# Seven products in place of eight for one more quarter of the fifth gate-and-up block

## The chip, the cores and the metric

The kernel runs on one NeuronCore of one Trainium2 chip. The metric is the device time of one execution in microseconds, taken as the median of several runs. TensorE (PE) multiplies matrices, VectorE (DVE) and ScalarE (ACT) do the elementwise work, GpSimd (POOL) issues some of the DMAs, and SyncE (SP) issues most of them.

## The reference

One layer of a streaming encoder on 256 rows of width 2048, all in 32-bit floats: a gated feed-forward network (FFN), a mixing part (a state-space group beside an attention group), a second FFN and a gated embedding. The change touches the first FFN's gate and up products only:

```python
def rms_norm(x, gain):
    xf = x.astype(jnp.float32)
    y = xf * lax.rsqrt(jnp.mean(xf * xf, axis=-1, keepdims=True) + EPS)
    return (y * gain.astype(jnp.float32)).astype(x.dtype)

def swiglu(h, w_gate, w_up, w_down):
    return (jax.nn.silu(h @ w_gate) * (h @ w_up)) @ w_down

x = x + 0.5 * swiglu(rms_norm(x, ffn1_norm[i]), ffn1_w_gate[i], ffn1_w_up[i], ffn1_w_down[i])
```

Here h is 256 x 2048 and each of w_gate and w_up is 2048 x 5632.

## The kernel before

**Blocks and quarters.** `ffn` goes over the 5632 columns in 11 blocks of 512 (`f` = 0 to 10). A block needs, for gate and for up, the product of 256 rows (two tiles `t` of 128) with 2048 x 512 weights. The depth of 2048 is taken in four quarters of 512 rows; one DMA of 1 MB brings a quarter of one weight into a `raw` buffer (five of them, in turn).

**Split operands.** Each operand is written as a high and a low part. ACT casts a half of a quarter (256 rows of depth) to the high part `whi`, and DVE subtracts to get the low part `wlo` (`split`, L182 and L185). For each 128 rows of depth PE adds three matmuls: high times high, low activations times high weights, high activations times low weights. A half of a quarter for both row tiles is thus 2 x 2 x 3 = 12 matmuls of 128 x 128 by 512 columns. `weight_pair` hands out the pairs of `whi` and `wlo`: four of them before the seventh block.

**Plain blocks.** `gemm_block` runs the four quarters of gate, then the four of up, each half by `gemm_half` (L353, L358), and calls `step()` after each half: 16 steps in a block.

**Seven products.** For one quarter, gate and up taken together form a 2 x 2 arrangement of weight blocks (`b11`, `b21` the two halves of gate's quarter, `b12`, `b22` those of up's). The two row tiles and the two halves of depth form the other 2 x 2 arrangement, and the kernel multiplies the two with seven block products in place of eight, each of six matmuls (L539, L542, L544 in `Seven.multiply`). That needs sums of the weight blocks on DVE (`t1`, `t2`, `t4`, L550), one sum `b12 + b22` that an accumulating DMA on POOL's queue makes in place (L578), sums of activations made once per quarter (`sum_forms`), and additions of the results at the end. `Seven.single` is the form that uses single banks of accumulators: products 1, 6 and 7 share one bank, so that the bank is copied out to `one` (L585, on ACT) before product 6 begins in it, and `six` (L595) and `seven` (L114, the line of `put_off`) are formed on DVE from it. In the blocks named in `alone`, the first quarter goes through `single` and the other three through `column`, gate first, then up: 4 + 6 + 6 = 16 steps as well. After gate's columns `gated` adds up the gate (L723, L726; the activation on ACT is L724). After up's columns `ended` adds the double bank of products 3 and 8 (L752) and multiplies gate and up (L754, twice). In a plain block that last multiplication is L792, twice.

**What comes beside.** `step()` advances every generator in `beside` once: the state-space preparation `s5_prep` (its lines are some 900 to 1160: L1087 to L1131 on DVE, L1115 on PE, coefficient loads L1071 and stores L1143 on POOL's queue), and whatever `put_off(n, ...)` has set for n steps later. In a block by sevens `ended` is put off to the next step, which is the first step of the block after it.

**Buffers.** `com("sg")` is one buffer of 1024 columns, `com("h")` two. In a block by sevens `sg` holds first the copy `one` and then the gate, and `h` the two halves of up. PSUM gives four single banks (`acc`) and two double ones (`aux`); the preparation's small products also use `aux`.

**Order.** Each engine runs its instructions in one order that the framework's scheduler fixes when the kernel is built; `pin` keeps program order for some of them, and `tc.issue_after` sets one behind another.

```python
early = 6 if bg else 0
alone = (3, 5) if bg else ()
```

So in the first FFN blocks 0, 1, 2 and 4 are plain, 3 and 5 have one quarter by sevens, and 6 to 10 have two by `chunk`. `f` counts from 0, and the text counts blocks from one: `f` = 3, 4, 5 are the fourth, fifth and sixth block.

Of the kernel before, what the change touches and what calls it, by code (L numbers as in the profile page):

```python
# [33 lines left out]
def layer_kernel(ctx: ExitStack, tc: tile.TileContext, a: dict, shapes: dict, out: bass.AP):  # L34
# [290 lines left out]
    @contextmanager  # L325
    def sums_phase(name):
        with phase(name) as pool:
            yield pool
            ring[0] = None
# [345 lines left out]
    def ffn(i, xn, nxt, bg=None):  # L675
# [1 line left out]
        hT = []  # L677
        pools = ExitStack()
        early = 6 if bg else 0
        alone = (3, 5) if bg else ()  # L680
        sevens = pools.enter_context(sums_phase(f"sums{i}"))
        hp = pools.enter_context(phase(f"h{i}"))
        side = ExitStack()
# [927 lines left out]

    n1, nm, n2, npl = Normed("ffn1_norm", load_turned), Normed("mix_norm"), Normed("ffn2_norm", kinds="hhnn", late=0), Normed("ple_norm", late=0)
    ffn(1, n1, nm, s5_prep)

    w_in = a["w_in"]
# [75 lines left out]
    mix.close()  # L1691

    ffn(2, n2, npl)


# [254 lines left out]
```

## Time and profile before

| what | value |
|---|---|
| median of 3 runs | 1808.87 us |
| lowest, highest | 1808.36, 1809.96 us |
| profiled execution | 1808.1 us |
| its span | 1806.3 us |
| matmuls | 8890, PE busy 1799.4 us |
| DVE busy | 1615.7 us |
| ACT busy | 1083.6 us |
| weights' and other bytes moved | 430.49 MB, mean 238 GB/s |

The span is the time from the first to the last instruction of the program; the run's time has 1.8 us around it. Busy times of PE count a matmul from its start to its modelled end, and matmuls overlap: their pace is read from the distance of their starts. Rows of the timeline begin with the start in us from the span's start and the duration; a bracket at the end gives the engine's idle time before the instruction and what ended it. In the rows of windows, a number in brackets counts the instructions. The fifth block begins on PE at 181.10 us and the sixth at 225.67 us.

### The profile page before, as it was taken

The page shows a single profiled execution, that of the slowest core. Times are in us where ns is not written, and L with a number is a line of the kernel's source. Part 1 is how long each engine was busy: PE and PEld are TensorE (multiplying, and loading weights), DVE is VectorE, ACT ScalarE, POOL GpSimd, SP SyncE. Part 2 cuts the span into 40 slices and gives each one's busy share as a digit, 9 for nine tenths or more (in the row PEclk, how much of TensorE's full clock was granted, in tenths as well). Part 3 has the DMA queues.
Part 4 walks back from the last instruction along what each step waited for, and adds up shares of the span by engine and source line. Part 5 has one row for each costly group of instructions (what it writes and reads, how often), then busy time and mean ns, then how long its engine had stood idle before and what let it go on. Part 6 is the DMA issues. An engine that isn't in the chain of part 4 may idle for free.

```text
span 1806.3 us, 24268 instructions
## 1 busy us (share of the span) xinstructions
PE 1799.4 (100%) x8890; PEld 1492.0 (83%) x8890; DVE 1615.7 (89%) x1894; ACT 1083.6 (60%) x1263; POOL 134.6 (7%) x196
## 2 busy tenths in 40 slices
PE   9999999999999999999999999999999999999998
PEld 7888888888888888888898888888888888888887
DVE  7998889999999898887867899999999999989875
ACT  7445455555566666466895566555565566666664
POOL 0020100000000001122121000000000000000000
PEclk9999999999999999999999999999999999999999
DMA  9689967687776667765646777776767786666663
GB/s 377 215 280 312 278 219 235 237 273 216 262 253 225 209 245 230 254 243 182 202 153 209 242 284 239 262 261 228 234 233 240 244 273 242 233 210 220 208 245 128
DMA packets 108518, 430.49 MB, mean 238 GB/s; under 512 B 24592, under 2 KB 48432, under 8 KB 66000
## 3 DMA queue, kind: packets, MB, share of 16 engines
q1 hardware_dynamic: 95952, 390.10, 61.1%
q0 software_dynamic: 12160, 38.55, 9.9%
q8 instruction: 69, 1.13, 0.3%
q14 instruction: 49, 0.40, 0.1%
q10 hardware_dynamic: 288, 0.31, 0.1%
HBM read 372.41 MB, written 10.88 MB: 212 GB/s over the span
## 4 chain that ended last, share of the span: by engine, by line
PE 99%; DMA 0%; DVE 0%; ACT 0%; SPq 0%; issue 0%; DVEq 0%; ACTq 0%
PE acc L358 31%; PE acc L353 16%; PE aux L358 15%; PE aux L353 8%; PE acc L539 5%; PE acc L544 5%; PE acc L542 5%; PE aux L544 4%; PE aux L539 4%; PE aux L542 4%; PE aux L1328 0%; PE acc L1585 0%; PE acc L1580 0%; PE acc L1576 0%; DMA raw<-in_head 0%; PE aux L1273 0%
## 5 line engine op out<-in xcount | busy, mean ns | idle before, releaser
L185 DVE TENSOR_TENSOR wlo<-raw,whi 128x1024 fp32r<-128x1024 f32 x478 | 576.4, 1221 | 94.0 <-ACT whi L182 90.7
L182 ACT CAST whi<-raw 128x1024 fp32r<-128x1024 f32 x478 | 495.8, 1050 | 271.2 <-PE acc L358 156.6
L358 PE MATMUL acc<-whi,nhi 128*128 128x512 f32 x852 | 332.7, 392 | 1.0 <-ACT whi L281 0.9
L358 PE MATMUL acc<-whi,nlo 128*128 128x512 f32 x852 | 330.4, 389 | 0.0
L353 PE MATMUL acc<-wlo,nhi 128*128 128x512 f32 x852 | 241.3, 390 | 0.0
L185 DVE TENSOR_TENSOR slo<-raw,shi 128x1024 fp32r<-128x1024 f32 x186 | 226.4, 1217 | 11.6 <-ACT shi L182 11.3
L182 ACT CAST shi<-raw 128x1024 fp32r<-128x1024 f32 x186 | 195.2, 1049 | 51.5 <-DMA raw<-in_ffn_w_down 24.0
L358 PEld LDWEIGHTS acc<-whi,nhi 128*128 128x128 f32 x852 | 159.8, 188 | 35.4 <-ACT whi L281 1.5
L353 PEld LDWEIGHTS acc<-wlo,nhi 128*128 128x128 f32 x852 | 159.7, 188 | 33.8 <-DVE wlo L185 0.4
L182 ACT CAST whi<-sum 128x1024 fp32r<-128x1024 f32 x83 | 87.5, 1054 | 166.2 <-DVE sum L550 154.4
L358 PEld LDWEIGHTS acc<-whi,nlo 128*128 128x128 f32 x852 | 159.9, 188 | 32.6 <-DVE nlo L282 0.2
L182 ACT CAST shi<-sum 128x1024 fp32r<-128x1024 f32 x61 | 64.3, 1053 | 103.8 <-DVE sum L550 99.8
L643 POOL DMA_DIRECT2D raw<-raw x47 | 41.4, 880 | 1032.5 <-DVE sum L550 782.0
L550 DVE TENSOR_TENSOR sum<-sum,raw 128x1024 f32<-128x1024 f32 x96 | 117.1, 1220 | 0.9
L185 DVE TENSOR_TENSOR wlo<-sum,whi 128x1024 fp32r<-128x1024 f32 x83 | 101.2, 1222 | 3.1 <-ACT whi L182 2.2
L358 PE MATMUL aux<-whi,nhi 128*128 128x512 f32 x244 | 95.0, 389 | 0.0
L358 PE MATMUL aux<-whi,nlo 128*128 128x512 f32 x244 | 94.9, 389 | 0.0
L185 DVE TENSOR_TENSOR slo<-sum,shi 128x1024 fp32r<-128x1024 f32 x61 | 74.5, 1221 | 0.7
L353 PE MATMUL aux<-wlo,nhi 128*128 128x512 f32 x244 | 75.1, 389 | 0.0
L550 DVE TENSOR_TENSOR sum<-raw,raw 128x1024 f32<-128x1024 f32 x48 | 58.5, 1220 | 3.6 <-DMA raw<-in_ffn_w_down 3.4
L539 PE MATMUL acc<-whi,hhi 128*128 128x512 f32 x154 | 60.2, 391 | 0.0
L542 PE MATMUL acc<-whi,hlo 128*128 128x512 f32 x154 | 60.0, 389 | 0.0
(420 smaller groups left out, 3531.9 us busy)
## 6 DMA issues: line engine op xcount, KB each, us to landing
raw<-in_ffn_w_down SPq DMA_DIRECT2D x88, 1024.0 KB, 4.9
raw<-in_ffn_w_gate SPq DMA_DIRECT2D x87, 1024.0 KB, 7.4
raw<-in_ffn_w_up SPq DMA_DIRECT2D x87, 1024.0 KB, 5.6
raw<-in_w_in SPq DMA_DIRECT2D x32, 1024.0 KB, 5.2
raw<-raw POOLq DMA_DIRECT2D x50, 512.0 KB, 5.6
raw<-in_w_out SPq DMA_DIRECT2D x16, 1024.0 KB, 5.0
raw<-in_w_ple_gate SPq DMA_DIRECT2D x16, 1024.0 KB, 5.0
hT<-mid SPq DMA_DIRECT2D x160, 64.0 KB, 4.7
```

The costliest lines, as they stand in the source:

```text
L182: copy = nc.scalar.copy(hi, src)
L185: rest = nc.vector.tensor_tensor(out=lo, in0=src, in1=hi.bitcast(F32), op=ALU.subtract)
L353: nc.tensor.matmul(ps[t], lhsT=lh, rhs=lo[:, j, cols], start=False, stop=stop and j == 1)
L358: nc.tensor.matmul(ps[t], lhsT=(ahi, alo)[i][:, 2 * h + j, t * P : (t + 1) * P], rhs=hi[:, j, cols], start=start and j == 0 and i == 0, st ...
L539: nc.tensor.matmul(ps, lhsT=lh[j], rhs=hi[:, j], start=begin and j == 0, stop=False, skip_group_check=joined)
L542: nc.tensor.matmul(ps, lhsT=ll[j], rhs=hi[:, j], start=False, stop=False, skip_group_check=joined)
L544: nc.tensor.matmul(ps, lhsT=lh[j], rhs=lo[:, j], start=False, stop=z in final and j == 1, skip_group_check=joined)
L550: nc.vector.tensor_tensor(out=t, in0=x, in1=y, op=ALU.add)
L643: nc.gpsimd.dma_start(b12, b22, accum_op=ALU.add)
```

## The change

The block with `f` = 4 joins those whose first quarter goes through `single`. It then takes the branch of `f in alone`: `single` on quarter 0, `column(0, (1, 2, 3))`, `column(1, (1, 2, 3))`, `gated` and `ended` as in the fourth and sixth block, in place of `gate(gemm_block(...))`, `gemm_block(...)` and the two L792. Nothing else is edited.

```diff
         early = 6 if bg else 0
-        alone = (3, 5) if bg else ()
+        alone = (3, 4, 5) if bg else ()
```

## The prediction

> **What bounds the kernel now.** I read the page first: the span, the busy shares, the slices, the chain that ended last.
>
> ```profile
> span 1806.3 us, 24268 instructions
> PE 1799.4 (100%) x8890; PEld 1492.0 (83%) x8890; DVE 1615.7 (89%) x1894; ACT 1083.6 (60%) x1263; POOL 134.6 (7%) x196
> DVE  7998889999999898887867899999999999989875
> PE 99%; DMA 0%; DVE 0%; ACT 0%; SPq 0%; issue 0%; DVEq 0%; ACTq 0%
> ```
>
> TensorE is busy for 1799.4 of 1806.3 us and the chain is 99% PE: the sum of the matmuls is the time, and an edit counts only by the matmuls it removes and by the holes it makes between them. VectorE (DVE) is next. Then I cut the stretch around the edit at the block starts: fourth block, fifth (the one that changes), sixth.
>
> ```profile
> core 0: us, PE busy (x) PEld busy (x) DVE busy (x) ACT busy (x) POOL busy (x), PEclk, DMA share, GB/s
> 136.90:181.10 44.20, 44.20 (x315) 36.16 (x314) 38.72 (x48) 22.30 (x29) 4.40 (x9) 1.00 0.97 309
> 181.10:225.70 44.60, 44.60 (x258) 36.69 (x257) 37.65 (x45) 19.30 (x22) 5.33 (x10) 1.00 0.91 277
> 225.70:269.00 43.30, 43.30 (x251) 35.43 (x250) 38.18 (x43) 23.55 (x26) 1.43 (x2) 1.00 0.70 229
> 270.00:350.00 80.00, 80.00 (x355) 66.24 (x354) 77.34 (x75) 46.46 (x50) 3.52 (x4) 1.00 0.74 250
> ```
>
> PE is full in all of them, at a granted clock of 1.00. The fifth block has no products by sevens and takes 44.60 us, the sixth has seven of them and takes 43.30; each holds one insertion of 64 small matmuls of the preparation (the fourth holds two). The last row, of the blocks after, shows DVE at 77.34 of 80.00 us with PE still full: a nearly full DVE does not by itself stop PE.
>
> **The change part by part.** *Products removed.* In the fifth block one quarter of the depth, for gate and up together, is 4 halves of 12 matmuls = 48; it becomes 7 products of 6 = 42. The interval between matmuls is read from starts, not from the busy 0.39 us, because they overlap.
>
> ```profile
> 139.63 0.39 PE L539 MATMUL acc<-whi,nhi 128*128 128x512 f32 x1
> 140.99 0.39 PE L539 MATMUL acc<-whi,hhi 128*128 128x512 f32 x1
> ```
>
> One product of six takes 140.99 - 139.63 = 1.36 us, 0.227 per matmul. Six fewer: -1.36 us. The blocks above agree: 44.60 - 43.30 = 1.30. [...] Six matmuls at the load's 0.188 us would be 1.13 us, and by their busy time 2.34; the spacing lies between, and it decides.
>
> *VectorE work added.* Per-instruction times, from the rows of the neighbours:
>
> ```profile
> L185 DVE TENSOR_TENSOR wlo<-raw,whi 128x1024 fp32r<-128x1024 f32 x15 | 18.2, 1218 | 6.9 <-ACT whi L182 6.9
> L550 DVE TENSOR_TENSOR sum<-sum,raw 128x1024 f32<-128x1024 f32 x2 | 2.4, 1218 | 0.0
> L792 DVE SCALAR_TENSOR_TENSOR h<-acc,sm,sg x4: 741/746/750, 136.9 to 227.4; 128x512 f32<-128x512 f32 x4
> L595 DVE TENSOR_TENSOR h<-acc,sg x2: 652/652/652, 142.9 to 232.7; 128x512 f32<-128x512 f32 x2
> L114 DVE TENSOR_TENSOR h<-acc,h x2: 684/685/686, 149.5 to 235.6; 128x512 f32<-128x512 f32 x2
> L723 DVE TENSOR_TENSOR sg<-acc,h x2: 681/686/691, 165.9 to 252.9; 128x512 f32<-128x512 f32 x2
> L726 DVE TENSOR_TENSOR h<-acc,h x2: 1217/1218/1218, 167.6 to 254.7; 128x1024 f32<-128x1024 f32 x2
> L752 DVE TENSOR_TENSOR h<-aux,h x2: 1218/1218/1218, 182.3 to 269.9; 128x1024 f32<-128x1024 f32 x2
> ```
>
> Seven splits in place of four: 3 x 1.22 = 3.65. The sums t1, t2, t4: 3 x 1.22 = 3.66. The combination: L595 0.65, L114 0.69, two L723 1.37, L726 1.22, L752 1.22 = 5.15; the two closing multiplications are there before (L792) and after (L754) at 0.75 each. Together +12.5 us on DVE, some 11.5 by starts, as one such instruction starts about 1.13 us after another. ACT gains three casts of 1.05 us and one copy and has 25 us free in the block: nothing.
>
> The cover for the 12.5 us is DVE's idle time:
>
> ```profile
> DVE wlo L185 <- ACT whi L182: 7.7, 6, 1.5
> DVE t L1087 <- DMA bc<-in_ssm_bc: 1.6, 1, 1.6
> DVE wlo L185 <- PE aux L1115: 1.5, 1, 1.5
> ```
>
> These waits of DVE between 169 and 231 us sum to 10.8 us, 6.9 of them inside the block. They are no hardship: DVE has done all that four pairs of buffers allow, and waits for PE to free one. Work put there costs nothing. What is short, about 1.7 us and the 1.36 us by which PE needs things earlier, comes out of DVE's lead; preparation work that sits between the splits is not urgent and can slip. So I take 0 for volume, with bounds 0 and 6.9 us (only the block's own idle usable: a shortfall of 5.55, plus 1.36). Nearest is the row of the later blocks with 77.34 of 80.00 and no hole.
>
> *The start of a block after one by sevens.* This is where I expect the cost. A block by sevens leaves its last step (`ended`: L752, then two L754) to the first step of the block after it. The next block's `single` copies bank 1 into `sg` (L585) before its fourth product may overwrite the bank; `sg` is one buffer, so the copy must wait until the last L754 of the block before has read it. Today a plain block precedes each `single`, and only two L792 stand there. The rows at the sixth block's start:
>
> ```profile
> 225.64 1.22 DVE L1124 TENSOR_TENSOR t<-bt,coef 128x1024 f32<-128x1024 f32 x1
> 226.78 1.41 DVE L792 SCALAR_TENSOR_TENSOR h<-acc,sm,sg 128x512 f32<-128x512 f32 x2
> 228.18 1.05 ACT L182 CAST whi<-raw 128x1024 fp32r<-128x1024 f32 x1 [0.31 <-PE acc L542]
> 229.14 0.58 ACT L585 COPY sg<-acc 128x512 f32<-128x512 f32 x1
> 229.77 0.49 PE L539 MATMUL acc<-whi,hhi 128*128 128x512 f32 x1
> PEld acc L539 <- ACT sg L585: 0.3, 1, 0.3
> ```
>
> L792 ends at 228.19, the copy waits for the cast ahead of it on ACT until 229.14, ends at 229.72, and the fourth product follows at 229.77; PE's weight load waited 0.3 us for it and the matmuls lost about 0.13. There is no room left. [...]
>
> The rows at the start of the fifth block, where the closing step of the fourth runs:
>
> ```profile
> 179.93 2.50 DVE L1100 TENSOR_TENSOR t<-ce,s5s 128x512 f32<-128x512 f32 x4
> 182.34 1.22 DVE L752 TENSOR_TENSOR h<-aux,h 128x1024 f32<-128x1024 f32 x1
> 183.47 1.22 DVE L185 TENSOR_TENSOR wlo<-raw,whi 128x1024 fp32r<-128x1024 f32 x1
> 184.61 1.41 DVE L754 SCALAR_TENSOR_TENSOR h<-h,sm,sg 128x512 f32<-128x512 f32 x2
> 181.10 0.39 PE L358 MATMUL acc<-whi,nhi 128*128 128x512 f32 x1
> ```
>
> PE starts the block at 181.10, so the fourth product is due at 181.10 + 3 x 1.36 = 185.18. If DVE keeps this order, L754 ends at 186.02, the copy at about 186.7, and PE loses 1.57. Bounds: 0, if L752 follows PE's end at once and nothing stands between (then L754 ends near 183.9); 2.6, if a 1.05 us cast also stands before the copy. I take 1.57, the order shown. At the sixth block's start L752 comes ahead of what is there: +1.13 by starts, and another 1.13 if a split slips in as at 183.47, less up to 0.95 that the copy spends behind the cast today. So 0.2 to 2.3; I take 0.8, from the lower half, as the cast's wait can overlap.
>
> *The accumulating DMA.* One more 512 KB addition of the up weights on POOL's queue.
>
> ```profile
> 165.28 2.88 POOL L1071 DMA_DIRECT2D coef<-scr_coef  x6
> 195.51 0.96 POOL L1071 DMA_DIRECT2D coef<-scr_coef  x2 [27.35 <-DVE t L1124]
> 214.33 0.92 POOL L578 DMA_DIRECT2D raw<-raw  x1 [12.87 <-DVE vq L1090]
> 143.86 3.90 ACT L182 CAST whi<-raw 128x1024 fp32r<-128x1024 f32 x4 [3.31 <-DMA raw<-raw]
> DMA to landing us min/median/max: 10.2/10.9/11.7
> ```
>
> It takes 10.2 to 11.7 us to land. In the fourth block ACT waited 3.31 us for it without a hole on PE. Here POOL's queue is free from 168.2 to 195.5, and the seventh product is due at 181.10 + 6 x 1.36 = 189.3: issued by about 175 it is in time. Cost 0, bounds 0 and 2. SP's queue: the up quarter is fetched earlier, the number of fetches stays, and at a DMA share of 0.91 there is room.
>
> Sum: -1.36 + 1.57 + 0.8 = +1.0 us. The profiled execution, 1808.1 us with 1.8 around its span, would go to 1809.1; it lies 0.8 below the median of 1808.87, so as a median: **1809.9 us**. The measurement of this kernel tells about 0.2% (3.6 us) from no change, so this is "same".
>
> **The rivals.**
> - *Full gain.* Scheduling puts L752 and L754 directly behind PE's end, the copy is in time at both starts: 1808.87 - 1.36 = 1807.5. For it: the fourth and sixth blocks run with holes of 0.13 us at most. Against: the rows at 182.34 to 186.02.
> - *DVE becomes the bound* (slower). The 12.5 us find only the 6.9 us inside the block; PE waits 6.9 us for low parts of weights, by the end of the sixth block's products: 1808.87 - 1.36 + 6.9 = 1814.4. It decides when DVE's lead of some 8 us is used up and more than 5 us must be waited for. Against: DVE at 97% later, without a hole. [...]
> - *Late addition.* If t1 slides to 176 us, where DVE is idle, b12 lands near 189.6 and the seventh product starts some 2 us late, beside the stalls above: 1811.9.
> - Faster by over 0.2% would need another 2.2 us of holes to vanish; PE has hardly that in this stage.
>
> **How the numbers follow.** Forecast (one or both starts late, 1808.6 to 1811.5) 0.50; full gain 0.28; late addition 0.08; DVE the bound 0.10; anything else 0.04. Range: down to 1806.9, the full gain with the 0.5 us by which single runs lie under the median; up to 1813.2, both starts at their upper bounds (-1.36 + 2.6 + 2.3 = +3.5) and 0.8 for the spread of runs. The likeliest alone: 1808.6 to 1811.5. Faster 0.03, same 0.86, slower 0.11.
>
> **What would show it.** PE rows: 42 matmuls of L539 to L544 in the fifth block, the distance of block starts 43.2 plus a hole. The hole right before the fourth product at both starts, put down to ACT's L585; L754 ending less than 0.7 us before the fourth product is due. DVE's idle time in the block falling from 6.9 to near 0. L578 three times, its third landing before 188. Wrong if the copy is in time (full gain), or if the waits are for `wlo` and go on past the seventh product (DVE).

## The result, and the profile after

The changed kernel took 1813.19 us, the median of 12 runs (1811.42 to 1814.20), against 1808.41 us for 12 runs of the kernel before (1806.92 to 1809.96): a ratio of 1.0026, 95% interval [1.0018, 1.0034]. It is slower by a little more than the 0.2% that a measurement of this kernel tells from no change. The profiled execution took 1812.45 us. Its page first: span, busy shares, VectorE in 40 slices.

```profile
span 1810.6 us, 24277 instructions
...
PE 1801.3 (99%) x8884; PEld 1492.3 (82%) x8884; DVE 1626.5 (90%) x1906; ACT 1085.1 (60%) x1267; POOL 135.2 (7%) x197
...
DVE  7999999999999898887867899999999999989875
```

Six matmuls are gone (8890 to 8884) and DVE has 10.8 us more to do, yet the span grew by 4.3 us. PE's busy time grew with it, by 1.9 us, though it has less to do: some matmuls must stand further apart. The stretches by block, cut at the starts of fourth, fifth, sixth and seventh block and 42 us on (columns as in the prediction: length, busy time and instructions of PE, PEld, DVE, ACT and POOL, granted clock, DMA share, GB/s):

```profile
136.20:180.30 44.10, 44.10 (x316) 36.06 (x315) 42.02 (x51) 22.39 (x29) 5.36 (x10) 1.00 0.99 310
180.30:224.00 43.70, 43.70 (x251) 35.23 (x250) 39.91 (x46) 22.38 (x26) 5.33 (x10) 1.00 0.79 265
224.00:268.00 44.00, 43.09 (x250) 35.12 (x249) 41.91 (x48) 23.72 (x25) 1.44 (x2) 1.00 0.78 248
268.00:310.00 42.00, 40.06 (x171) 32.61 (x170) 38.02 (x38) 21.61 (x24) 1.68 (x2) 0.96 0.70 238
```

The fifth block now has the sixth's number of matmuls (251). PE (first number behind the comma) has no idle time in it, 0.91 us in the sixth block, and 1.94 us in the last row, which no step of the prediction speaks of; there the granted clock fell to 0.96. PE's waits between 180 and 330 us, the total, the number and the longest:

```profile
PE acc L539 <- ACT shi L182: 1.9, 1, 1.9
...
PE acc L539 <- ACT sg L585: 0.9, 1, 0.9
...
PEld acc L539 <- ACT sg L585: 1.7, 2, 1.3
```

The copy to `sg` (L585) is what it waited for at the two starts, and the weight loads (PEld) with it. The larger wait is for `shi`, the high part of a sum of weight blocks. The timeline around the three places:

```profile
181.53 1.22 DVE L752 TENSOR_TENSOR h<-aux,h 128x1024 f32<-128x1024 f32 x1
...
183.80 1.41 DVE L754 SCALAR_TENSOR_TENSOR h<-h,sm,sg 128x512 f32<-128x512 f32 x2
...
185.24 0.59 ACT L585 COPY sg<-acc 128x512 f32<-128x512 f32 x1
...
185.88 0.50 PE L539 MATMUL acc<-whi,hhi 128*128 128x512 f32 x1
...
217.97 1.22 DVE L550 TENSOR_TENSOR sum<-raw,raw 128x1024 f32<-128x1024 f32 x1
...
219.96 0.92 POOL L578 DMA_DIRECT2D raw<-raw  x1 [11.19 <-DVE sum L550]
...
227.26 1.41 DVE L754 SCALAR_TENSOR_TENSOR h<-h,sm,sg 128x512 f32<-128x512 f32 x2
...
229.04 1.05 ACT L182 CAST whi<-raw 128x1024 fp32r<-128x1024 f32 x1 [1.37 <-DMA raw<-raw]
...
230.00 0.57 ACT L585 COPY sg<-acc 128x512 f32<-128x512 f32 x1
...
230.62 0.50 PE L539 MATMUL acc<-whi,hhi 128*128 128x512 f32 x1 [0.92 <-ACT sg L585]
...
268.72 1.22 DVE L752 TENSOR_TENSOR h<-aux,h 128x1024 f32<-128x1024 f32 x1 [0.24 <-PE aux L353]
...
270.99 1.41 DVE L754 SCALAR_TENSOR_TENSOR h<-h,sm,sg 128x512 f32<-128x512 f32 x2
...
272.32 1.22 DVE L550 TENSOR_TENSOR sum<-sum,raw 128x1024 f32<-128x1024 f32 x1
...
273.62 1.04 ACT L182 CAST shi<-sum 128x1024 fp32r<-128x1024 f32 x1 [5.63 <-issue]
...
274.71 0.50 PE L539 MATMUL acc<-shi,nhi 128*128 128x512 f32 x1 [1.94 <-ACT shi L182]
```

At the fifth block's start L754, the copy and product 6 stand one right behind the other (the last L754 ends at 185.21, the copy starts at 185.24), as predicted; product 6 is 0.15 us late. At the sixth block's start another wait ends last. There L754 was done at 228.67, and product 6 was due at 229.55, so a copy of 0.57 us right behind L754 would have been in time. But on ACT the copy stands behind a cast, and this cast waited for the sixth block's accumulating DMA (`raw<-raw`), which was issued at 219.96 and landed at 228.94. In the kernel before, that DMA went out at 214.33: it waits for `t1`, which DVE made 5.4 us earlier there.

```profile
212.54 1.22 DVE L550 TENSOR_TENSOR sum<-raw,raw 128x1024 f32<-128x1024 f32 x1
```

DVE did not lack the time for `t1` in the new kernel: its weights had landed at 212.76, and DVE was idle for 2.12 and 1.49 us ahead of the two splits that stand before it. `t1` has a later place in DVE's order.

The third group is the seventh block. DVE is not late there, since it waits 0.24 us for PE before L752; but it makes `t4` (L550) only after it has ended the sixth block. ACT has been idle for 5.63 us when it can cast `t4`, and product 4 begins 1.94 us late. In the kernel before, DVE made `t4` ahead of that end:

```profile
265.20 2.48 DVE L550 TENSOR_TENSOR sum<-sum,raw 128x1024 f32<-128x1024 f32 x2
...
268.44 1.06 ACT L182 CAST shi<-sum 128x1024 fp32r<-128x1024 f32 x1
...
269.90 1.22 DVE L752 TENSOR_TENSOR h<-aux,h 128x1024 f32<-128x1024 f32 x1
```

The two L550 of the first row are `t2` and `t4`; `t4` is ready at 267.7 and cast at 268.44, with no wait of PE.

To put sizes on this, take every matmul of 512 columns and add up by how much the distance to the next start exceeds 0.227 us (distances that exceed it by less than 0.013 us are left out). The whole difference of the spans is then there:

| lost PE time, us | before | after | difference |
|---|---|---|---|
| start and rest of the fifth block (183.5 to 227) | 0.22 | 0.78 | +0.56 |
| sixth block (227 to 266) | 0.32 | 1.39 | +1.07 |
| seventh and start of the eighth (266 to 330) | 0.00 | 3.81 | +3.81 |
| everywhere else | 6.2 | 6.5 | +0.3 |

+5.7 us of these and -1.36 us of removed products make +4.3. Of the 3.81, 2.2 are the wait for `t4`, and 1.6 the matmuls right behind it, which stood up to 0.427 us apart.

### The profile page after: what moved, and what is told of

Same layout as the page of the kernel before. It is cut to its first block, busy times and chain, and to the rows that moved or that the text cites. A ratio compares the mean times of both kernels' runs of the same rounds, so it can differ in the third digit from the quotient of the medians.

```text
span 1810.6 us, 24277 instructions
## 1 busy us (share of the span) xinstructions
PE 1801.3 (99%) x8884; PEld 1492.3 (82%) x8884; DVE 1626.5 (90%) x1906; ACT 1085.1 (60%) x1267; POOL 135.2 (7%) x197
## 4 chain that ended last, share of the span: by engine, by line
PE 94%; DVE 2%; DMA 2%; issue 1%; ACT 1%; SPq 1%; POOL 0%; ACTq 0%; DVEq 0%; POOLq 0%
PE acc L358 29%; PE acc L353 15%; PE aux L358 14%; PE aux L353 7%; PE acc L539 5%; PE acc L544 5%; PE acc L542 5%; PE aux L544 3%; PE aux L542 3%; PE aux L539 3%; DMA raw<-in_ffn_w_down 1%; SPq L233 1%; DMA raw<-raw 0%; DVE wlo L185 0%; PE aux L1328 0%
## 5 line engine op out<-in xcount | busy, mean ns | idle before, releaser
L358 PE MATMUL acc<-whi,nhi 128*128 128x512 f32 x812 | 317.4, 393 | 0.1
L358 PE MATMUL acc<-whi,nlo 128*128 128x512 f32 x812 | 314.8, 389 | 0.0
L353 PE MATMUL acc<-wlo,nhi 128*128 128x512 f32 x812 | 231.3, 389 | 0.0
L358 PEld LDWEIGHTS acc<-whi,nhi 128*128 128x128 f32 x812 | 152.5, 188 | 32.6 <-issue 0.5
L353 PEld LDWEIGHTS acc<-wlo,nhi 128*128 128x128 f32 x812 | 152.4, 188 | 31.7
L358 PEld LDWEIGHTS acc<-whi,nlo 128*128 128x128 f32 x812 | 152.6, 188 | 31.1
L550 DVE TENSOR_TENSOR sum<-sum,raw 128x1024 f32<-128x1024 f32 x98 | 119.5, 1220 | 0.9
L185 DVE TENSOR_TENSOR wlo<-sum,whi 128x1024 fp32r<-128x1024 f32 x86 | 105.0, 1221 | 5.6 <-ACT whi L182 4.8
L358 PE MATMUL aux<-whi,nhi 128*128 128x512 f32 x268 | 104.5, 390 | 0.0
L358 PE MATMUL aux<-whi,nlo 128*128 128x512 f32 x268 | 104.3, 389 | 0.0
L353 PE MATMUL aux<-wlo,nhi 128*128 128x512 f32 x268 | 82.5, 389 | 0.0
L550 DVE TENSOR_TENSOR sum<-raw,raw 128x1024 f32<-128x1024 f32 x49 | 59.7, 1219 | 6.3 <-DMA raw<-in_ffn_w_down 5.4
```

The costliest lines, as they stand in the source:

```text
L185: rest = nc.vector.tensor_tensor(out=lo, in0=src, in1=hi.bitcast(F32), op=ALU.subtract)
L353: nc.tensor.matmul(ps[t], lhsT=lh, rhs=lo[:, j, cols], start=False, stop=stop and j == 1)
L358: nc.tensor.matmul(ps[t], lhsT=(ahi, alo)[i][:, 2 * h + j, t * P : (t + 1) * P], rhs=hi[:, j, cols], start=start and j == 0 and i == 0, st ...
L550: nc.vector.tensor_tensor(out=t, in0=x, in1=y, op=ALU.add)
```

## The experiments

Each kernel was timed beside the kernel before on its chip. The table has, for every profile, the lost PE time as above (each of the first two columns holds some 0.2 us of the insertions of small matmuls), and where `t4` of the seventh block stands on DVE against the end of the sixth block. The lost time is that of one execution, the profiled one, which for e1 and e9 was the shortest of the kernel's runs and for e10 the longest (1812.69 us).

| kernel | median, us | minus before, us | ratio, 95% interval | lost 183.5 to 266 | lost 266 to 330 | `t4` |
|---|---|---|---|---|---|---|
| before | 1808.41 | | | 0.5 | 0.0 | ahead |
| after | 1813.19 | +4.8 | 1.0026 [1.0018, 1.0034] | 2.2 | 3.8 | behind |
| e1 | 1807.71 | -0.6 | 0.9998 [0.9989, 1.0008] | 0.9 | 0.0 | ahead |
| e2 | 1814.20 | +5.9 | 1.0031 [1.0020, 1.0042] | 3.8 | 2.9 | ahead |
| e3 | 1814.01 | +5.7 | 1.0032 [1.0019, 1.0045] | 4.2 | 2.2 | behind |
| e4 | 1809.38 | +1.1 | 1.0006 [0.9997, 1.0015] | 2.5 | 0.0 | ahead |
| e5 | 1807.24 | -0.7 | 0.9997 [0.9988, 1.0006] | 0.4 | 0.0 | ahead |
| e6 | 1813.62 | +5.7 | 1.0032 [1.0020, 1.0045] | 3.6 | 4.9 | behind |
| e7 | 1808.82 | +0.9 | 1.0006 [0.9997, 1.0014] | 2.0 | 1.1 | ahead |
| e8 | 1807.83 | -0.1 | 1.0004 [0.9995, 1.0013] | 1.1 | 1.1 | ahead |
| e9 | 1811.25 | +3.5 | 1.0024 [1.0014, 1.0034] | 1.9 | 2.2 | behind |
| e10 | 1810.33 | +2.6 | 1.0015 [1.0007, 1.0024] | 2.9 | 3.8 | behind |
| e11 | 1809.62 | +1.5 | 1.0008 [0.9999, 1.0017] | 4.5 | 0.0 | ahead (set) |
| e12 | 1808.50 | +0.3 | 1.0003 [0.9994, 1.0012] | 2.0 | 1.2 | behind (set) |

**The copy's wait taken away (e1), and the same in the kernel before (e5).** In the blocks by sevens the first product is copied into the single-purpose buffer `sq`, which is free there, and `sg` holds the gate alone. The copy then waits for no earlier block. e5 has the same edit in the kernel before.

```diff
+                one = com("sq") if f in alone else gate_cols[0]
+
-                def gated(s, g=gate_cols, u=up_cols, hh=hh):
-                    for z, (ps, other) in enumerate(((s.bank(2), g[0]), (s.bank(4), u[1]))):
+                def gated(s, g=gate_cols, u=up_cols, hh=hh, one=one):
+                    for z, (ps, other) in enumerate(((s.bank(2), one), (s.bank(4), u[1]))):
...
-                    s.single(0, gate_cols[0], *up_cols)
+                    s.single(0, one, *up_cols)
```

> The changed kernel with the copy of bank 1 (L585) written to another buffer (sq) than the gate's, so that it no longer waits for the two L754 of the block before. Theory A (each hole has its own cause: the copy behind L754 at the fifth and sixth block's start, and at the seventh block's start a split that is planned late): the holes at 185.5 (0.15 and 0.11), about 0.3 around 189 and 229.3 (1.08 and 0.11) go, some 1.5 us, and the 2.1 us at 272.4 with the slow matmuls after it stays: 1811.7 us. Theory B (VectorE has too much to do, and whatever is freed at one place is lost at the next wait): nothing or hardly anything, 1813 us, with the holes moved.

> The kernel before (fifth block plain) with the copy L585 written to the buffer sq. Theory A (the gain of the run with the copy in sq came from the wait that it takes away): here only the 0.13 us at the sixth block's start can go, 1808.2 us, no difference. Rival (the other buffer brings another plan that is better by itself): some 5 us as on the changed kernel, or at least 1.5, so 1806.8 us or less.

e1 is level with before (0.9998) and below what either theory gave it: with this one dependence the whole 4.8 us go, the seventh block's part too, which the expectation had left standing. More than a wait went: on ACT the copy now stands ahead of the cast that held it at the sixth block's start (it begins at 226.23), and DVE makes `t4` ahead of the sixth block's end. What is left of waits of PE between 180 and 330 us in e1, then its row of the seventh block's first part, and then that row of the kernel after:

```profile
PE acc L353 <- DVE wlo L185: 0.2, 1, 0.2
```

```profile
268.00:290.00 22.00, 22.00 (x98) 18.21 (x97) 20.89 (x21) 11.91 (x13) 0.89 (x1) 1.00 0.67 193
```

```profile
268.00:290.00 22.00, 20.06 (x82) 16.07 (x81) 20.84 (x21) 10.74 (x11) 0.89 (x1) 0.92 0.65 196
```

DVE is equally full in both (20.89 and 20.84 of 22.00 us); PE is full in the first and not in the second. So it is not the amount of VectorE work that costs. In e5, where no block by sevens follows another, the same edit brought nothing that can be told (0.9997 [0.9988, 1.0006]): the gain belongs to the change, not to the buffer.

**One start in place of two (e4).** `alone = (3, 4)`: the fifth block is by sevens, the sixth plain again.

> Sevens in the fourth and fifth block and not in the sixth: as many matmuls and as much VectorE work as before the change, but two such blocks in a row. Theory A: the start of the fifth block loses about 0.5 us, the sixth's start and the seventh's are as before: 1808.9 us. Theory B (volume): the same volume as before, 1808.4 us. A third reading, that any block by sevens right after another is what costs: half of what the change lost beside its products, (4.8 + 1.4) / 2 = 3.1, so 1811.5 us.

In the profile PE waited 1.5 us for L585 before product 6 (at 187.60), and nothing follows from it later. The median is 1.1 us above before, which the interval does not tell from nothing; the third reading's 1811.5 us is not borne out.

**Two other places for the work (e2, e3).** e2 lets the pairs of `sum` and weight buffers begin at the other end of their ring for the chunk blocks (`ring[:] = [self.turns, 6]`), e3 brings the second sums of activations one block forward (`(4, 11)` in place of `(5, 11)`).

> The changed kernel with the turn of the weight pairs begun at another place in the seventh block, so that the split of t1 takes one of the four old pairs and not the first of the new ones, whose memory the preparation gives back. Theory A: t4 no longer waits behind L754 for t1's buffer, the hole of 2.1 us at 272.4 and the 1.7 us of slow matmuls after it go: 1809.4 us, the holes of the fifth and sixth block stay. Theory B: VectorE is behind all the same, t4 is as late, 1813 us.

> The changed kernel with the 4.1 us of VectorE work of the second set of activation sums (L479, four L496, one L185) moved from the end of the sixth block to the end of the fifth. Theory A: the preparation ends no earlier, since more work stands ahead of it, and the hole at 272.4 stays: 1813 us or more. Theory B: VectorE has 4.1 us more where it is behind, the hole at 272.4 and the slow matmuls go: 1809.4 us.

Neither helped; e3 went as theory A said. e2 is a miss of some 5 us: the hole at product 4 of the seventh block went, but 2.5 us of waits for L585 at the starts and 2.9 us in the eighth block came. It also shows how a late start arises. DVE's order around the fifth block's start is that of the new kernel, but it was 1.12 us later (L752 at 182.65 in place of 181.53), after a wait of 1.63 us in the fourth block for a cast that follows the accumulating DMA, which landed 11.2 us after its issue there and 10.1 us in the new kernel, and after one of 1.65 us for a weights' DMA (0.85 us in the new kernel). L585 came 1.12 us later as well (186.36 for 185.24), and product 6 was held by about as much more (1.42 us where the new kernel has 0.15). How late the copy is thus followed the transfers: 1.12 us lie between these two profiles.

**t1's cast first (e6).** In the seventh block `t1` is cast ahead of `t2`, as in the kernel before; nothing else is forced.

```diff
+            first = self.last
...
-            self.product(6, summed(1), t2, final)
+            with ExitStack() as held:
+                if kb == 0 and self.ws[0][1] == 6 * NB and self.ws[0][0] is a["ffn1_w_gate"]:
+                    for ins in first:
+                        held.enter_context(tc.issue_after(ins))
+                self.product(6, summed(1), t2, final)
```

> The changed kernel with the split of t1 in the seventh block set ahead of the split of t2 on ACT and DVE, as it stands in the kernel before; nothing else. Theory A2 (the planned place of t1's split makes the hole at 272.4, the copy makes the two at the blocks' starts): 2.1 us go, 3.8 if the slow matmuls behind it go as well, and the starts keep 1.5 to 3.2: 1809.4 to 1811 us. Rival (VectorE is late by that much anyhow, from the holes before): the hole stays at some wait, 1813 us.

The cast of `t1` moved to 263.37 us, and the loss stayed, as the rival said. In hindsight the edit left the decisive thing as it was: `t4` was still made behind the end of the sixth block.

```profile
272.31 1.41 DVE L759 SCALAR_TENSOR_TENSOR h<-h,sm,sg 128x512 f32<-128x512 f32 x2
...
274.77 1.22 DVE L550 TENSOR_TENSOR sum<-sum,raw 128x1024 f32<-128x1024 f32 x1
...
276.07 1.04 ACT L182 CAST shi<-sum 128x1024 fp32r<-128x1024 f32 x1 [7.71 <-issue]
```

**Ending a block at once (e7, e8).** `ended` is not put off where the next block is by sevens too; e8 has this together with `sq`.

```diff
-                if f in alone:
+                if f in alone and f + 1 not in alone:
                     put_off(0, ended, s)
```

> The changed kernel with the closing step of the fourth and fifth block issued in their own block and not at the first step of the next. Theory A2: L585 still waits for the last L754, so the starts lose what they lost, 1.5 to 3.2; the plan has t1's split first again, so the seventh block's hole goes: 1809.4 to 1811 us. Rival (it is the putting off that makes L754 late): the starts' holes go too, 1808 us or less.

> Both: the copy in sq, and the closing step in its own block. Theory A2: no wait for L754 is left, and the six matmuls fewer show in full: 1808.3 - 1.36 - 0.13 = 1806.8 us, 0.1 to 0.9 below the run with the copy in sq alone. Rival (VectorE has no room left and each product saved is lost in waits for low parts): 1808 us or more.

e7 takes most of the loss away (+0.9), with 0.9 us of wait for L585 left at the fifth block's start and 0.8 us for `wlo` in the eighth. Its 1808.82 us lie between the two forecasts: the hole at the sixth block's start went, that at the fifth did not. Together with `sq` it adds nothing to e1; 1807.83 us again lie between theory and rival.

**One start freed at a time (e9, e10).** `one = com("sq") if bg and f == 3` in e9, and `f == 5` in e10. The first leaves both waits of the new kernel as they are; the second frees the sixth block's copy alone.

> The new kernel, but only the fourth block (f = 3) keeps its first gate product in a buffer of its own, so that the copy at L585 for the fifth block finds sg written and used... by no earlier block still at work, in short: of the two starts after a block by sevens one has its single buffer changed. The copy of f = 3 goes to sq, the copy of f = 4 to sg, the copy of f = 5 to sg after f = 4's. Since f = 3 still writes its sg at the end (its gated gate columns), f = 4's copy waits for it as in the new kernel; what changes is only that f = 3's own copy no longer opens sg. Theory (the wait of a block's copy for the block before is what costs): both start waits stay, so the time is that of the new kernel, 1811.5 to 1813.5, 2 to 3 us of holes at the two starts together and 2 us or more in the seventh and eighth blocks. Rival (what matters is that some first product is out of sg at all, by way of the planner's order): below 1809.5.

> The new kernel, but only the sixth block (f = 5) puts its first gate product into a buffer of its own (sq), so its copy at L585 no longer waits for the fifth block's last use of sg; the fifth block's copy waits for the fourth's as in the new kernel. Theory (the start of the sixth block is the one that makes the seventh and eighth late; the e4 kernel had a hole of 1.6 at the fifth block's start and nothing after it): a hole of 0.15 to 1.5 at 185, none by L585 at 230, at most 0.5 lost from 266 to 330, time 1807.8 to 1809.5. Rival (the late VectorE comes from the fifth block's own work, whatever the sixth block's start does): the seventh and eighth blocks still lose 1.5 us or more, time 1810 to 1811.5.

e9 went as the theory said in the seventh block (2.2 us lost there), with less at the starts (1.4 us where 2 to 3 were expected) and a time just under the range. In e10 the theory fell. The sixth block starts without a hole, and the seventh has exactly that of the new kernel, down to the slow matmuls behind it:

```profile
275.99 0.53 PE L539 MATMUL acc<-shi,nhi 128*128 128x512 f32 x1 [1.93 <-ACT shi L182]
276.33 0.62 PE L542 MATMUL acc<-shi,nlo 128*128 128x512 f32 x1
276.75 0.63 PE L539 MATMUL acc<-shi,nhi 128*128 128x512 f32 x1
```

e10's median of 1810.33 us and the loss in the seventh block are what the rival gave. Its reason, a late VectorE, is not what the traces show: in after, e3, e9 and e10 alike DVE waits for PE (0.2 to 0.8 us) right before it begins to end the sixth block, and the same hole of 1.9 us follows. That points to a fixed order of instructions, counted from PE's own end of the sixth block, not to a delay that is carried along.

**The order in the seventh block, set by hand (e11, e12).** e11 is the new kernel with the end of the sixth block put behind `t4` on DVE; up to that place DVE's order is unchanged. e12 is e1 with `t4` put behind that end.

```diff
 e11
+                    with tc.issue_after(Seven.added) if bg and f == 5 else ExitStack():
                         nc.vector.tensor_tensor(out=hh, in0=s.banks[3.8], in1=hh, op=ALU.add)
...
-                    put_off(0, ended, s)
+                    put_off(1 if f == 5 else 0, ended, s)
 e12
+            with tc.issue_after(Seven.ended[1]) if kb == 0 and Seven.ended[0] == 5 else ExitStack():
                 t4 = self.add(t2, b21)
```

`Seven.added` is the latest L550 and `Seven.ended[1]` the last multiplication of the first FFN's block before.

> The new kernel with one thing forced in the seventh block: t4's addition (L550) stands on VectorE ahead of the end of the sixth block (the addition at L752 and the two products at L754), as it does in the kernel before; up to that place the planned order is the new kernel's, after it the planner goes on by itself. Theory P (the hole of 2.1 us at product 4 of the seventh block is that planned order: t4 stands behind the block's end on VectorE, and its cast is late): the hole at 272 to 274 is at most 0.3, the two start holes (0.1 to 1.6 each) stay, time 1809.4 to 1811.2. Rival Q (VectorE is simply late there, whatever the order): what is put behind t4 is late in its turn, 1.5 us or more is lost between 266 and 330 at other waits, time 1812 to 1814.

> The counterpart: the kernel with the first product in sq (no wait at the starts), with t4's addition in the seventh block forced behind the end of the sixth block, as the new kernel has it. Theory P: a hole of 0.8 to 2.1 us at product 4 of the seventh block though both starts are free, time 1808.4 to 1810 where e1 had 1807.7. Rival Q (without late starts VectorE has the time): at most 0.3 us of hole there, time 1807.2 to 1808.3.

Of e11 and then of e12, in three fences each: DVE's order on the timeline, the seventh block's first part, and the longest of PE's waits from 180 to 330 us.

```profile
271.69 1.22 DVE L550 TENSOR_TENSOR sum<-sum,raw 128x1024 f32<-128x1024 f32 x1
272.83 1.22 DVE L752 TENSOR_TENSOR h<-aux,h 128x1024 f32<-128x1024 f32 x1
```

```profile
268.00:290.00 22.00, 22.00 (x98) 18.22 (x98) 21.78 (x21) 12.78 (x14) 0.89 (x1) 1.00 0.60 188
```

```profile
PE acc L539 <- ACT sg L585: 3.2, 2, 1.8
```

```profile
269.65 1.41 DVE L756 SCALAR_TENSOR_TENSOR h<-h,sm,sg 128x512 f32<-128x512 f32 x2
...
270.98 1.22 DVE L550 TENSOR_TENSOR sum<-sum,raw 128x1024 f32<-128x1024 f32 x1
```

```profile
268.00:290.00 22.00, 21.06 (x93) 17.14 (x92) 21.06 (x21) 11.39 (x12) 0.89 (x1) 1.00 0.73 209
```

```profile
PE acc L539 <- ACT shi L182: 0.9, 1, 0.9
```

In e11 nothing is lost in the seventh block, though both starts were later than in the new kernel (3.2 us of waits for L585) and DVE came to the sixth block's end 4.1 us later (L752 at 272.83 for 268.72, in part by the edit itself). In e12 PE is idle for 0.9 us at product 4, though it waited for no copy at either start; the hole is smaller because the split of 1.1 us that stands between L752 and L754 in the new kernel does not stand there. The interval of e11, [0.9999, 1.0017], ends below that of the new kernel, if by little ([1.0018, 1.0034]), so the order's part of the loss is seen in the times; that of e12 overlaps that of e1, and its hole is read from the profile alone. All the profiles of the table divide the same way: `t4` behind, and PE is idle for 0.9 to 1.9 us before product 4 of the seventh block; `t4` ahead, and it is not. (What e2, e7 and e8 lose past 266 us lies in the eighth block.)

So the loss has two parts, and both go when the copy has a buffer of its own: the starts themselves, and a planned order that changed further on, in a block that the edit does not touch. By the medians over before the order is worth about 3.3 us (after +4.8, e11 +1.5) and the starts about 2 (e11 +1.5, e1 -0.6), the latter within what the intervals leave open.

The two starts are not alike. At the fifth the copy began 0.03 to 0.04 us after the last L754's end in all nine profiles in which it waited for the fourth block. At the sixth, in the six profiles that lose there (after, e2, e3, e6, e9, e11), L754 had been done for 1.1 to 3.4 us; what ended last was the cast ahead of the copy, which began 0.1 us after the accumulating DMA had landed. In e10 that DMA landed at 232.20, later than in the new kernel, but the copy stood ahead of the cast, and nothing was lost there. So at the sixth start too the planned order decides, on ACT, together with a late addition.

What in the scheduler's reckoning turned the orders is open; for the seventh block, freeing one of the two copies (e10) did not turn `t4` back, freeing all three (e1) did, and so did a plain sixth block (e4).

## Where the prediction held and where it failed

The measured 1813.19 us lie within the range by 0.01 us, and that is luck. The upper end, 1813.2, was worked out from both starts at their upper bounds (+3.5) and 0.8 for the spread; the two starts cost 1.6, and 3.8 came from a block that the sum does not have. The forecast of 1809.9 and its own span, 1808.6 to 1811.5, were missed. (The lower end adds up to 1807.0, not 1806.9, which changes nothing.)

*Products removed, -1.36 us: right by the profile.* The matmuls are 8884. The fifth block lasts 43.82 us from start to start (180.29 to 224.11) after 44.57, and 43.82 holds the 0.56 of new holes. The times do not show the gain: e1's median lies 0.6 below before and e5's, without the change, 0.7, and neither interval tells that from nothing. e1's span is 1.8 us below that of before, but 0.8 of it is less loss outside these blocks.

*VectorE work added, taken as 0: right for its volume.* DVE took 2.3 us more in the fifth block's row, 3.3 more in the fourth's and 3.7 more in the sixth's, so the work spread over the neighbours' idle time; 3.8 us of idle time stayed in the fifth block, where near 0 was forecast. e1 does all of it and loses only 0.4 us more than before in these blocks. The rival that DVE becomes the bound gave a time near the measured one, 1814.4, by another mechanism: in the new kernel PE's matmuls waited for no low part between 180 and 330 us (1.9 us for `shi`, 0.9 us for the copy), and its weight loads 0.6 us for low parts. By busy time in the sixth block's row, 41.91 of 44.00 us against 35.12 of weight loading, DVE would be the bound; e1 takes no work from DVE, and the loss went.

*Start of the fifth block, +1.57: the mechanism right, the size not.* DVE kept the order shown to the hundredth: L754 ended 4.92 us after the block's start (185.21 - 180.29), as in the estimate (186.02 - 181.10). What changed is PE's order. Not 18 matmuls but 24 stood ahead of product 6, so that it was due 1.36 us later than the estimate had it, and 0.15 us were lost; the rest of the block lost 0.4. In other profiles with 24 matmuls there L752 came later and more was lost, up to 2.0 us (e11); where the copy goes to `sq` (e1), 18 stand ahead again.

*Start of the sixth block, +0.8: 1.07 measured, near it by luck.* L754 was in time there. *The accumulating DMA, taken as 0,* is what cost it: right for the fifth block's, issued at 163.62 and landed 10 us later, ahead of 188, and wrong for the sixth block's, whose cast at 229.04 held the copy. It is in kind the rival of the late addition, given 0.08, but one block further on and at product 6 in place of 7.

*The step that failed is the sum.* It ends with the sixth block's start and puts all later blocks at nothing. It costs the added instructions in an order taken from before, and assumes that the plan stays. The plan was made anew, and `t4` behind the sixth block's end cost 2.2 us of hole and 1.6 us of slower matmuls in the profiled execution: 3.8 of the 4.3. The forecast is therefore 3.3 us short, and "same", within 3.6 us, was given 0.86 where the time came out 4.8 us slower.

## What to carry to other kernels

When an edit makes a buffer's next writer wait for the step that ended the block before, look for the single buffer first: a second home for one value took the whole loss away here. When a scheduler orders the engines, compare the planned order of each engine far beyond the edit before trusting a sum over the edited stage; a sum of weights that was made behind another block's closing step, two blocks on, cost more than both starts. An estimate of when an instruction is due needs the order of its own engine too: six matmuls moved ahead of product 6 made one hole a tenth of its forecast. A wait that the profile puts down to a copy does not say what the copy waited for: here it was a different thing at each of two starts. And the same hole to a tenth of a microsecond in kernels with different delays is a sign of order, not of lateness.

## What the runs showed of the hardware

The holes of 1.9 us in the seventh block were followed by slow matmuls in two of four profiles. With the same hole, e10 and e9, in the 4 us that follow it:

```profile
276.00:280.00 4.00, 4.00 (x11) 3.13 (x12) 4.00 (x5) 4.00 (x5) 0.00 (x0) 0.57 0.76 281
```

```profile
276.00:280.00 4.00, 4.00 (x19) 3.28 (x18) 4.00 (x5) 4.00 (x6) 0.00 (x0) 1.00 0.74 274
```

In the first the granted clock is 0.57 and 11 matmuls fall into the 4 us, most of them 0.427 us apart; in the second it is 1.00 with 19. After is like the first (0.57 from 275 to 279 us), e3 like the second (1.00 from 276 to 284 us). The slow stretch lasted 3 to 4 us and cost 1.6 us beyond the hole in both e10 and after. In e3 PE was also idle for 3.0 us before the sixth block's product 6 (at 233.19), and the granted clock was 1.00 over the stretch from 225.7 to 269 us. What lowers the clock behind the same hole in two profiles and not in the two others is not shown: the idle time was 1.93 us in e10 and in e9, 1.94 us in after and in e3. The 12 runs of the kernel after lie in two groups, three at 1811.4 to 1811.5 and nine at 1812.5 to 1814.2; that the clock divides them is not shown: the mean granted clocks are 0.999 to 1.000 in the three and 0.998 to 1.000 in the nine.
